# Channel sums of the RMS norms and of RWKV's bonus: data as weights against a matrix of ones as weights

## The chip, the cores and the metric

One NeuronCore of one Trainium2 chip runs the whole program. The metric is the device time of one execution in microseconds (us), as the median of several runs.

## The reference

The input x has 256 tokens of 1024 channels. Two layers follow one another. In each layer the input is RMS-normalised and modulated by a condition vector, and one combined projection feeds three branches whose gated outputs are merged, projected and added to x:

```
h = rms_norm(x, norm_pre) * (1 + scale) + shift
p = h @ w_in
o_mla  = attention on two RMS-normalised compressed projections (512 and 256 channels)
o_rwkv = RWKV-7: delta-rule state over heads of 64 channels, then
         y = group_norm(y) * ln_w + ln_b
         bonus = sum over a head's 64 channels of (r * k * r_k), times v
         y = y + bonus
o_gla  = gated linear attention, 4 heads of 256 value channels, each RMS-normalised
merged = sigmoid(gate_a)*o_mla + sigmoid(gate_b)*o_rwkv + sigmoid(gate_c)*o_gla
x = x + gate * rms_norm(merged @ w_out, norm_post)
```

## The kernel before

Activations stand channel-major: 128 channels in the partitions, the 256 tokens along a row. A weight matrix comes by DMA in tiles of 128x1024 float32 (`weights`, L333). ScalarE rounds each tile to a part `hi` that one TensorE pass carries exactly (L344), VectorE subtracts to get the rest `lo` (L345), and `dense` (L349) makes three products hi*hi, hi*lo, lo*hi for each 128x128 block (L358). `dense_pair` does this for 256 output columns. These products are most of TensorE's work.

The program is written layer by layer: RWKV's preparation `rw_prep` for half of the heads (L463), RWKV's chain over eight chunks of 32 tokens `rw_chain` (L562), GLA (`gla`, L821), `rw_prep` and `rw_chain` for the other half, MLA (`mla`, L910), and `finish` (L1069). The TileContext is opened with `schedule_with_timeline_sim=True`: when the program is built, a scheduler orders the instructions of each engine by a timing model of its own, and each engine then runs its list strictly in that order. So parts that stand far apart in the source run side by side (GLA beside the first chain, MLA beside the second), and an instruction that has to wait holds up all that stands behind it in its engine's list. PSUM has eight banks in three pools: `ps_d` (3, dense products), `ps_c` (2, RWKV's chain), `ps_m` (3, everything else).

At the head of a chain stands a triangular solve. `gram` products (L574) are masked into `Gm` (L581), go through DRAM (`bd`, `Bb`, L591 to L598), and GpSimd solves 31 columns, each by a product `tm` and a sum `Xb` (L607, L610). `Xb` goes through DRAM (`xd`, `Xs`, L612 to L618; ScalarE issues these DMAs) and the chain over the chunks can begin (`u`, L692).

Sums over channels, that is over partitions, are made by TensorE. Before, `sums` (L141) takes the data as the weights, 128 tokens at a time, and a column of ones (`one_b`), or two half columns (`halfsel`), as what moves: the result has tokens in the partitions and a column or two for each block of channels. The places:

- `start` (L268, once): 8 blocks of squares into `ss` (L281).
- `rw_prep` (L525 to L555, 4 times): 4 blocks into `bonp` (L535), copied to `bon` (L554). The sums of squares `ssk` (L517) are made in the same way.
- `gla` (L889, for each of 4 heads, in 2 layers): the head's squares `gsq`, whose two tiles GpSimd adds first (L888), into `gss`. After the last head come one square root, one reciprocal (L891, L892).
- `compress` in `mla` (L941): 2 blocks for the 512 channels (`cq`), 1 for the 256 (`ckv`), into `sscq` and `ssckv`; `rms_row` (L397) reduces them, takes the root and the reciprocal (L400 to L402).

To come back to channel-major, `to_rows` (L146) splits the result in two parts on VectorE (L149, L150), turns both on TensorE (L153, `ptr...`), copies the rows out on ScalarE (L157); and `spread` or `spread2` (L160, L164) multiplies a row by a column of ones so that it stands in all partitions (`ri`, `gbc`, `bc`; the PSUM results). `spread2` does so for the two heads of 64 channels in a tile. The consumers read that PSUM tile: `xn` (L285), `og` (L901), `cx` (L946), and at the end of a chain `bv` (L753), which GpSimd adds to `orw` (L755).

Of the kernel before, what the change touches and what calls it, by code (L numbers as in the profile page):

```python
# [20 lines left out]
P = 128  # L21
# [13 lines left out]
# Column slots of w_in, 256 columns each (see _w_in_columns).  # L35
# [7 lines left out]
# Columns of the packed per-channel parameters, one per 128 channels.  # L43
# [6 lines left out]
# Order of the column tiles of ada_w: shift and scale of the same channels side by side.  # L50
# [11 lines left out]
def _turn_pieces():  # L62
    """frac(2^k / 2 pi) for the steps of the pieces of an angle, each as a 12-bit part and the rest."""
    from fractions import Fraction

    pi = Fraction(314159265358979323846264338327950288419716939937510, 10 ** 50)
    out = []
    for k in (20, 9, -2):
        f = Fraction(2) ** k / (2 * pi)
        f -= round(f)  # L70
        hi = Fraction(round(f * 4096), 4096)
        out.append((k, float(hi), float(np.float32(float(f - hi)))))
    return out, float(np.float32(float(1 / (2 * pi))))
# [3 lines left out]
def trunk(  # L77
# [35 lines left out]
    pick = const.tile([16, 5], F32R, name="pick")  # L113
# [9 lines left out]
    # running sums start again at every 32nd or 64th token  # L123
# [12 lines left out]
    gneps = cut(1)  # L136
    A.copy(pick8, cut(8)[0:16].unsqueeze(2).broadcast_to([16, 8, 64]))
    A.copy(pick, cut(5)[0:16])
    pick4, pick1 = pick[0:8, 0:4], pick[0:2, 4:5]

    def sums(ps, src, sel):  # L141
        """ps [128, 2, n]: sums over channels of src [128, 256 tokens], tokens in the partitions."""
        for half in range(2):
            PE.matmul(ps[:, half], src[:, half * P:(half + 1) * P], sel, start=True, stop=True)

    def to_rows(pool, src, n, nm):  # L146
        """[2 n, 256]: src [128, 2, n], given for tokens, turned and in two parts that one pass carries."""
# [12 lines left out]
    def spread(ps, rows, j, sel):  # L160
        """ps [128 channels, 256] = row j, both parts."""
        PE.matmul(ps, sel[:, j:j + 1].broadcast_to([sel.shape[0], P]), rows, start=True, stop=True)

    def spread2(ps, rows, j):  # L164
        """Row j to the first 64 channels, the next to the others."""
# [81 lines left out]
    def interleave():  # L247
        """Part of the modulation that is wanted later, between two weight transfers."""
# [5 lines left out]
    def ada_part(L, l, slots, pool=None):  # L254
        """Two columns of the modulation for each slot, 128 channels each, before its bias."""
# [12 lines left out]
    def start(L, hl, firsts, order):  # L268
        """The first layer's input and its first products of it, 128 channels at a time as their
        modulation comes in."""  # L270
# [5 lines left out]
        ss = ps_m.tile([P, 2, KD], F32, tag="m", name="ss0")  # L276
        for s in range(4):
            sq = pp.tile([P, 2, T], F32, tag="sq", name="sq0", bufs=2)
            A.activation(sq, xn[:, 2 * s:2 * s + 2], AF.Square)
            for i in range(2):  # L280
                sums(ss[:, :, 2 * s + i:2 * s + i + 1], sq[:, i], one_b)  # L281
# [51 lines left out]
    def weights(src, name, n=2048, pool=None, sub=None):  # L333
        """Both parts of n columns of a slot, in tiles of CHUNK columns."""
# [14 lines left out]
    def dense(ps, w, kt, i, act):  # L349
        """ps [128 columns, 256 tokens] = W[:, column tile i].T @ activations; a tile's rows side by side."""  # L350
# [13 lines left out]
    def dense_tok(ps, w, kt, n, act, st):  # L364
        """ps [128 tokens, n columns] = activations.T @ W; a row's columns side by side."""
# [22 lines left out]
    def split(hi, lo, src, scale=None):  # L388
        """src (times scale) as the sum of two parts that one pass each carries exactly."""
# [7 lines left out]
    def rms_row(pool, ss, inv, nm):  # L397
        """[128, 256] 1 / rms of the tokens, in every partition; ss [128, 2, n] parts of the sums of squares."""
        r = pool.tile([P, 2, 1], F32, tag="rr", name=f"rr{nm}", bufs=2)
        V.tensor_reduce(r[:, :, 0], ss, AX.X, ALU.add)  # L400
        A.activation(r, r, AF.Sqrt, scale=inv, bias=eps6)
        V.reciprocal(r, r)  # L402
        rows = to_rows(pool, r, 1, nm)
        ps = ps_m.tile([P, T], F32, tag="m", name=f"ri{nm}")
        spread(ps, rows, 0, pick1)
        return ps

# [1 line left out]
    def norm_rows(pp, parts, nm):  # L409
        """1 / rms of the rows of a [128, 1024] given in parts."""  # L410
# [25 lines left out]
    def prenorm(L, hl, pp, xr, i):  # L436
        """128 rows of x, normalised and modulated, channel-major in two parts."""
# [4 lines left out]
        for half in range(2):  # L442
            ps = ps_c.tile([P, 4, P], F32, tag="c", name="ps_t")
            for k in range(4):
                # turned and normalised
# [17 lines left out]
    def rw_prep(L, l, qp, h, sh):  # L463
# [4 lines left out]
        R.GC = rw.tile([P, 4, 8], F32, tag="GC", name=f"GC{l}{qp}")  # L468
        n = f"{l}{qp}"
        with tc.tile_pool(name=f"rp{n}", bufs=1, side="right", reuse_waits="tile") as rp:  # L470
# [9 lines left out]
            for s in range(2):  # L480
# [5 lines left out]
                # two products at a time, in either half of the PE array's rows  # L486
# [38 lines left out]
            bonp = ps_m.tile([P, 2, 8], F32, tag="m", name="bonp")  # L525
            for s in range(2):
                g2 = slice(2 * s, 2 * s + 2)
                ps = dense_pair(win[l, S_RR[qp] + s], f"rr{n}{s}", h)
                br = rp.tile([P, 2, T], F32, tag="t2", name="br", bufs=3)
                for i in range(2):  # L530
# [4 lines left out]
                    sums(bonp[:, :, 2 * g:2 * g + 2], br[:, i], halfsel)  # L535
# [12 lines left out]
                # what the state loses comes first for the first pair of heads and last for the other  # L548
# [4 lines left out]
            bon = rp.tile([P, 2, 8], F32, name="bon")  # L553
            A.copy(bon, bonp)  # L554
            R.bon = to_rows(rw, bon, 8, f"bon{n}")  # L555
            for s in range(2):
                ps = dense_pair(win[l, S_RV[qp] + s], f"rv{n}{s}", h)
                for i in range(2):
                    shifted(L, R.vs[:, 2 * s + i], ps[:, i], "mu_v", qp * 4 + 2 * s + i)
        return R  # L560

    def rw_chain(L, l, qp, R, orw, rc):  # L562
        n = f"{l}{qp}"
        # A head is (gh, g2, qi).  Partitions of what is token-major: (g2, half, token of a chunk); the
        # removals of the pair of heads gh are in the half gh, its queries and values in the other.
        Gm = rc.tile([P, 8, 2, 2, 64], F32, name="Gm")
        for c4 in range(2):
            # heads in different rows of the PE array write different banks
# [16 lines left out]
        # The unit triangular systems of all chunks and heads of this half: one (row parity,  # L585
        # chunk, head) in each partition, solved column by column.
# [34 lines left out]
        # The states of two heads stand block-diagonally, as do the values.  # L621
# [12 lines left out]
        # four heads at a time, each in rows and columns of the PE array of its own  # L634
        pairs = [(g2, gh) for g2 in range(2) for gh in range(2)]

        def by_token(ch):
            """A chunk's decayed keys and its values, turned; the values into their blocks."""
# [23 lines left out]
        for ch in range(8):  # L662
# [4 lines left out]
            def of_state(ps, s):  # L667
                """What each pair's removals (s = 0) or queries read of the state."""
# [6 lines left out]
            def of_chunk(ps, s, r, g2, gh, qi):  # L675
                """... and of the chunk's tokens in the rows r."""
# [49 lines left out]
        # group norm over the 64 values of a head  # L726
# [21 lines left out]
        for s in range(2):  # L748
            bc = ps_c.tile([P, 2, T], F32, tag="c", name="bc2")
# [546 lines left out]
```

## Time and profile before

| | |
|---|---|
| three runs | 1183.28, 1189.07, 1191.8 us |
| median | 1189.07 us |
| span of the profiled execution, first to last instruction | 1181.3 us |
| TensorE matmul, weight load | 93%, 85% of the span |
| VectorE, ScalarE, GpSimd | 68%, 49%, 40% of the span |
| chain that ended last: TensorE, GpSimd, VectorE, DMA | 58%, 16%, 9%, 8% |

The profile names engines PE (TensorE matmuls), PEld (its weight loads, beside the matmuls), DVE (VectorE), ACT (ScalarE), POOL (GpSimd), SP (SyncE). A row of a group of instructions has line, engine, operation, out<-in, shapes, count, then busy us and mean ns of one, then the idle time before them. The profiled execution's own time is its span and what the launch puts around it; that is not listed apart, and the three runs lie 2.0 to 10.5 us above the span.

### The profile page before, as it was taken

What the parts mean: (1) busy time and instruction counts of PE and PEld (TensorE: products, weight loads), DVE (VectorE), ACT (ScalarE), POOL (GpSimd) and SP (SyncE); (2) the same over time, 40 slices, a digit from 0 to 9 for tenths busy, and PEclk for the clock granted to TensorE, in tenths of its full rate; (3) what the DMA queues carried; (4) which work ended last, traced back from release to release, by engine and by line L of the source; (5) the groups of instructions that cost most, each with busy time, mean ns of one, the idle gap of its engine ahead of it and who ended that gap; (6) DMA issues with size and microseconds to landing.
All of it is one profiled execution on the core that took longest, in us unless ns stands there. A gap on an engine that the chain in (4) does not pass through costs nothing.

```text
span 1181.3 us, 25207 instructions
## 1 busy us (share of the span) xinstructions
PE 1103.1 (93%) x10365; PEld 1001.9 (85%) x10365; DVE 799.6 (68%) x1220; ACT 578.8 (49%) x980; POOL 466.6 (40%) x609
## 2 busy tenths in 40 slices
PE   5799898999999599999989999899999969999997
PEld 3798887988999477999989889789899968799997
DVE  6978754766986667677665685367677665667774
ACT  4357233545547243554556834255384635446452
POOL 7955338324536643103100536523063753211210
PEclk7799998999999899999999989999999989999999
DMA  9665753465466443547654245334444542234761
GB/s 353 215 200 167 176 154 117 131 219 153 144 220 216 128 143 103 120 151 231 207 182 150 83 153 161 107 90 133 146 141 138 181 123 91 81 120 142 249 210 40
DMA packets 70066, 185.15 MB, mean 157 GB/s; under 512 B 24608, under 2 KB 25120, under 8 KB 69824
## 3 DMA queue, kind: packets, MB, share of 16 engines
q1 hardware_dynamic: 48304, 173.37, 46.3%
q10 hardware_dynamic: 21648, 10.18, 3.4%
q8 instruction: 81, 1.33, 0.5%
q14 instruction: 33, 0.27, 0.1%
HBM read 179.32 MB, written 4.20 MB: 155 GB/s over the span
## 4 chain that ended last, share of the span: by engine, by line
PE 58%; POOL 16%; DVE 9%; DMA 8%; issue 5%; ACT 4%; ACTq 1%; DVEq 0%; SPq 0%; POOLq 0%
PE ps_gt L358 10%; PE ps_wo L358 9%; POOL tm L607 5%; POOL Xb L610 5%; PE ps_rz L358 4%; PE y L371 3%; PE ps_gz L358 3%; PE ps_gq L358 2%; PE ps_mz L358 2%; PE ps_rk L358 2%; PE ps_rv L358 2%; DMA wr_wout<-in_wout_dram 2%; DMA Bb<-bd 1%; DMA adaw<-in_ada_dram 1%; PE sp L702 1%
## 5 line engine op out<-in xcount | busy, mean ns | idle before, releaser
L358 PE MATMUL ps_gt<-hhi,lo_gt 128*128 128x256 f32 x384 | 109.9, 286 | 0.1
L358 PE MATMUL ps_gt<-hhi,hi_gt 128*128 128x256 f32 x384 | 109.7, 286 | 0.0
L358 PE MATMUL ps_gt<-hlo,hi_gt 128*128 128x256 f32 x384 | 109.0, 284 | 0.0
L345 DVE TENSOR_TENSOR lo_gt<-wr_gt,hi_gt 128x1024 fp32r<-128x1024 f32 x48 | 63.4, 1322 | 40.1 <-ACT hi_gt L344 39.6
L345 DVE TENSOR_TENSOR lo_wo<-wr_wo,hi_wo 128x1024 fp32r<-128x1024 f32 x48 | 67.2, 1399 | 31.3 <-ACT hi_wo L344 31.1
L263 DVE SCALAR_TENSOR_TENSOR adaw<-adaw,cb 128x1024 f32<-128x1024 f32 x48 | 70.7, 1476 | 15.1 <-DMA adaw<-in_ada_dram 14.8
L344 ACT CAST hi_gt<-wr_gt 128x1024 fp32r<-128x1024 f32 x48 | 50.4, 1049 | 54.9 <-PE ps_gt L358 20.1
L344 ACT CAST hi_wo<-wr_wo 128x1024 fp32r<-128x1024 f32 x48 | 50.4, 1050 | 51.0 <-PE ps_gt L358 25.1
L358 PEld LDWEIGHTS ps_gt<-hhi,lo_gt 128*128 128x128 f32 x384 | 73.4, 191 | 1.5 <-DVE lo_gt L345 0.4
L358 PEld LDWEIGHTS ps_gt<-hhi,hi_gt 128*128 128x128 f32 x384 | 73.6, 192 | 1.0 <-issue 0.2
L712 POOL TENSOR_TENSOR gst<-ST,GC 64x256 f32<-64x256 f32 x48 | 39.0, 813 | 88.8 <-DVE ST L716 75.0
L358 PEld LDWEIGHTS ps_gt<-hlo,hi_gt 128*128 128x128 f32 x384 | 73.5, 191 | 0.6 <-issue 0.2
L607 POOL TENSOR_TENSOR tm<-Xb,Bb 128x126 f32<-128x126 f32 (+22 forms) x124 | 64.8, 523 | 22.9 <-DMA Bb<-bd 13.7
L785 POOL TENSOR_TENSOR merged<-merged,tg 128x512 f32<-128x512 f32 x14 | 24.6, 1758 | 122.6 <-DVE tg L784 108.9
L610 POOL TENSOR_TENSOR Xb<-Xb,tm 128x126 f32<-128x126 f32 (+22 forms) x124 | 61.0, 492 | 9.5
L643 POOL COPY bks<-vs 128x128 f32<-128x128 f32 x32 | 11.1, 346 | 131.4 <-PE ptok L650 125.4
L654 ACT COPY vals<-ptok 32x128 f32<-32x128 f32 x128 | 32.9, 257 | 46.7 <-PE ptok L650 34.2
L344 ACT CAST hi_gz<-wr_gz 128x1024 fp32r<-128x1024 f32 x16 | 16.8, 1048 | 50.6 <-PE ps_gz L358 18.8
L696 DVE COPY vals<-u 32x128 f32<-32x128 f32 x128 | 36.5, 286 | 7.0 <-PE u L692 5.1
L371 PE MATMUL ps_gv<-hi_gv,hhi 128*128 128x256 f32 x128 | 36.5, 289 | 3.4 <-ACT hi_gv L344 2.3
L358 PE MATMUL ps_gz<-hhi,hi_gz 128*128 128x256 f32 x128 | 39.6, 309 | 0.0
L358 PE MATMUL ps_gz<-hhi,lo_gz 128*128 128x256 f32 x128 | 39.3, 307 | 0.0
(492 smaller groups left out, 4358.9 us busy)
## 6 DMA issues: line engine op xcount, KB each, us to landing
adaw<-in_ada_dram SPq DMA_DIRECT2D x48, 512.0 KB, 3.8
wr_gt<-in_win_dram SPq DMA_DIRECT2D x48, 512.0 KB, 3.9
wr_wo<-in_wo_dram SPq DMA_DIRECT2D x48, 512.0 KB, 3.8
wr_rk<-in_win_dram SPq DMA_DIRECT2D x16, 512.0 KB, 5.1
wr_rr<-in_win_dram SPq DMA_DIRECT2D x16, 512.0 KB, 4.5
wr_rv<-in_win_dram SPq DMA_DIRECT2D x16, 512.0 KB, 4.2
wr_gv<-in_win_dram SPq DMA_DIRECT2D x16, 512.0 KB, 4.4
wr_gz<-in_win_dram SPq DMA_DIRECT2D x16, 512.0 KB, 4.2
```

What stands on the lines that cost most here:

```text
L263: V.scalar_tensor_tensor(w, w, 0.5, cb, ALU.mult, ALU.mult, accum_out=L.mod[:, ADA_ORDER[2 * s + i]:ADA_ORDER[2 * s + i] + 1],)
L344: A.copy(hi, wr)
L345: (sub or V).tensor_sub(lo, wr, hi.bitcast(F32))
L358: PE.matmul(ps if len(a.shape) == 2 else ps.rearrange("p (a b) -> p a b", a=2), wt[:, at + k * P:at + (k + 1) * P], a, start=i == 0, stop= ...
L371: PE.matmul(ps, a[:, st * P:(st + 1) * P] if len(a.shape) == 2 else a[:, st], wt[:, k * n % CHUNK:k * n % CHUNK + n], start=i == 0, stop=i ...
L607: G.tensor_mul(tv, Xb[:, 0:nr, m:m + 1].broadcast_to([P, nr, w]), Bb[:, m:m + 1, m + 1:32].broadcast_to([P, nr, w]))
L610: G.tensor_add(Xb[:, 0:nr, m + 1:32], Xb[:, 0:nr, m + 1:32], tv)
L654: A.copy(vals[ch % 2][rows(g2, 1 - gh), :, gh, g2], pt[32 * g:32 * g + 32, 2].rearrange("p (q v) -> p q v", q=2))
L696: V.tensor_copy(val[rows(g2, gh), :, gh, g2], u[rows(g2, gh)])
L702: PE.matmul(sp[chan(qi), 2 * gh:2 * gh + 2].rearrange("p g v -> p (g v)"), tk[:, gh, chan(qi)], val[:, qi, gh].rearrange("p g v -> p (g v) ...
L712: G.tensor_mul(gst[chan(qi)], ST[chan(qi), :, qi], R.GC[chan(qi), :, ch:ch + 1].broadcast_to([64, 4, 64]))
L785: (V if b == 2 and s == 3 else G).tensor_add(m, m, tg)
```

## The change

Two square matrices stand ready as weights: `ones`, all ones, and `twos`, block-diagonal ones in two blocks of 64. The new `all_sums` takes them as weights and the data, 256 tokens, as what moves. The result has the sum in every channel (or in the 64 channels of its head) at once, so that turning and spreading fall away. Per-row roots and reciprocals become 128x256 ones, and `rms_row` returns an SBUF tile instead of a PSUM one. In GLA each head has its own root and reciprocal, made inside the loop over heads. In `rw_prep` the bonus sums are copied to `R.bon`, 128x512 at a time, and GpSimd multiplies them by the values at the end of `rw_prep`; the end of the chain only adds them. The squares of the keys (`ssk`, `rn`) still go by `sums`, `to_rows` and `spread2`. Comments are dropped.

```diff
-    pick = const.tile([16, 5], F32R, name="pick")
+    ones = const.tile([P, P], F32, name="ones")
+    G.memset(ones, 1.0)
...
+    twos = const.tile([P, P], F32, name="twos")
+    A.copy(twos.rearrange("p (a b) -> p a b", a=2), halfsel.unsqueeze(2).broadcast_to([P, 2, 64]))
     A.copy(pick8, cut(8)[0:16].unsqueeze(2).broadcast_to([16, 8, 64]))
-    A.copy(pick, cut(5)[0:16])
-    pick4, pick1 = pick[0:8, 0:4], pick[0:2, 4:5]
...
+    def all_sums(ps, src, sel, first=True, last=True):
+        PE.matmul(ps, sel, src, start=first, stop=last)
...
-    def spread(ps, rows, j, sel):
-        PE.matmul(ps, sel[:, j:j + 1].broadcast_to([sel.shape[0], P]), rows, start=True, stop=True)
...
-        ss = ps_m.tile([P, 2, KD], F32, tag="m", name="ss0")
+        ss = ps_m.tile([P, T], F32, tag="m", name="ss0")
...
-                sums(ss[:, :, 2 * s + i:2 * s + i + 1], sq[:, i], one_b)
+                all_sums(ss, sq[:, i], ones, s + i == 0, s + i == 4)
...
-    def rms_row(pool, ss, inv, nm):
-        r = pool.tile([P, 2, 1], F32, tag="rr", name=f"rr{nm}", bufs=2)
-        V.tensor_reduce(r[:, :, 0], ss, AX.X, ALU.add)
-        A.activation(r, r, AF.Sqrt, scale=inv, bias=eps6)
+    def rms_row(pool, ss, inv, nm, bufs=2):
+        r = pool.tile([P, T], F32, tag="rr", name=f"rr{nm}", bufs=bufs)
+        A.activation(r, ss, AF.Sqrt, scale=inv, bias=eps6)
         V.reciprocal(r, r)
-        rows = to_rows(pool, r, 1, nm)
-        ps = ps_m.tile([P, T], F32, tag="m", name=f"ri{nm}")
-        spread(ps, rows, 0, pick1)
-        return ps
+        return r
...
+        R.bon = rw.tile([P, 4, T], F32, tag="bon", name=f"bon{l}{qp}")
...
-            bonp = ps_m.tile([P, 2, 8], F32, tag="m", name="bonp")
             for s in range(2):
...
+                bonp = ps_m.tile([P, 2, T], F32, tag="m", name="bonp")
                 for i in range(2):
...
-                    sums(bonp[:, :, 2 * g:2 * g + 2], br[:, i], halfsel)
+                    all_sums(bonp[:, i], br[:, i], twos)
+                A.copy(R.bon[:, g2], bonp)
...
-            bon = rp.tile([P, 2, 8], F32, name="bon")
-            A.copy(bon, bonp)
-            R.bon = to_rows(rw, bon, 8, f"bon{n}")
             for s in range(2):
                 ps = dense_pair(win[l, S_RV[qp] + s], f"rv{n}{s}", h)
                 for i in range(2):
                     shifted(L, R.vs[:, 2 * s + i], ps[:, i], "mu_v", qp * 4 + 2 * s + i)
+                g2 = slice(2 * s, 2 * s + 2)
+                G.tensor_mul(R.bon[:, g2], R.bon[:, g2], R.vs[:, g2])
...
         for s in range(2):
-            bc = ps_c.tile([P, 2, T], F32, tag="c", name="bc2")
-            for i in range(2):
-                spread2(bc[:, i], R.bon, 2 * (2 * s + i))
-            bv = rc.tile([P, 2, T], F32, tag="vb", name="bv", bufs=2)
-            V.tensor_mul(bv, R.vs[:, 2 * s:2 * s + 2], bc)
             o = orw[:, qp * 4 + 2 * s:qp * 4 + 2 * s + 2]
-            G.tensor_add(o, o, bv)
+            G.tensor_add(o, o, R.bon[:, 2 * s:2 * s + 2])
...
-        ss = ps_m.tile([P, 2, 4], F32, tag="m", name="gss")
+        rns = []
...
-            sums(ss[:, :, hd:hd + 1], sq[:, 0], one_b)
-        rn = gp.tile([P, 2, 4], F32, name="grn")
-        A.activation(rn, ss, AF.Sqrt, scale=1.0 / 256, bias=eps6)
-        V.reciprocal(rn, rn)
-        rn = to_rows(gp, rn, 4, f"g{l}")
+            ss = ps_m.tile([P, T], F32, tag="m", name="gss")
+            all_sums(ss, sq[:, 0], ones)
+            rns.append(rms_row(gp, ss, 1.0 / 256, f"g{l}{hd}", 4))
...
-            bc = ps_m.tile([P, T], F32, tag="m", name="gbc")
-            spread(bc, rn, hd, pick4)
             for dt in range(2):
-                V.scalar_tensor_tensor(o[:, dt], o[:, dt], L.p("gla_norm", dt), bc, ALU.mult, ALU.mult)
+                V.scalar_tensor_tensor(o[:, dt], o[:, dt], L.p("gla_norm", dt), rns[hd], ALU.mult, ALU.mult)
...
-                ss = ps_m.tile([P, 2, npair], F32, tag="m", name=f"ss{nm}")
+                ss = ps_m.tile([P, T], F32, tag="m", name=f"ss{nm}")
...
-                    sums(ss[:, :, s:s + 1], sq[:, 0], one_b)
+                    all_sums(ss, sq[:, 0], ones, s == 0, s == npair - 1)
```

## Rows read from the trace of the kernel before

**Rows 1.** The page: busy time of each engine; the chain by engine.
```profile
PE 1103.1 (93%) x10365; PEld 1001.9 (85%) x10365; DVE 799.6 (68%) x1220; ACT 578.8 (49%) x980; POOL 466.6 (40%) x609
...
PE 58%; POOL 16%; DVE 9%; DMA 8%; issue 5%; ACT 4%; ACTq 1%; DVEq 0%; SPq 0%; POOLq 0%
```
**Rows 2.** Stretches: length, busy of PE, PEld, DVE, ACT, POOL; granted clock; DMA.
```profile
20.00:30.00 10.00, 4.69 (x13) 2.76 (x13) 9.67 (x11) 3.09 (x4) 10.00 (x7) 0.50 0.99 372
...
200.00:210.00 10.00, 7.15 (x40) 6.95 (x39) 4.34 (x8) 7.26 (x9) 3.58 (x12) 0.68 0.49 146
...
400.00:410.00 10.00, 5.43 (x25) 4.86 (x26) 7.50 (x9) 2.61 (x4) 5.30 (x10) 0.58 0.23 71
...
960.00:970.00 10.00, 4.32 (x28) 3.57 (x29) 8.16 (x13) 4.60 (x10) 2.11 (x3) 0.57 0.52 132
```
**Rows 3.** The waits: total us, times, longest.
```profile
PE ps_uv L371 <- ACT kn L991: 11.5, 1, 11.5
...
ACT kn L991 <- POOL Xb L610: 11.7, 1, 11.7
...
PE gss L144 <- POOL gsq L888: 9.6, 3, 4.3
```
**Rows 4.** The chain in order of time, TensorE's small groups: start, us, what.
```profile
213.22 0.54 PE ptrg L153 x4
...
216.62 0.32 PE gbc L162
...
859.93 0.86 PE pw L489 x4
...
869.92 0.43 PE bc L166 x2
...
891.66 1.88 PE bonp L144 x16
...
897.12 0.54 PE ptrbon L153 x4
```
**Rows 5.** Groups of DVE by line and shape.
```profile
L901 DVE SCALAR_TENSOR_TENSOR og<-og,par,gbc 128x256 f32<-128x256 f32 x16 | 6.6, 474 | 1.6 <-PE gbc L162 1.6
...
L753 DVE TENSOR_TENSOR bv<-vs,bc 128x512 f32<-128x512 f32 x8 | 5.4, 680 | 0.0
...
L946 DVE SCALAR_TENSOR_TENSOR cx<-cx,par,ricq 128x256 f32<-128x256 f32 x8 | 3.3, 474 | 2.1 <-PE ricq L162 2.1
...
L523 DVE RECIPROCAL rn<-rn 128x16 f32<-128x16 f32 x4 | 1.0, 240 | 0.0
...
L892 DVE RECIPROCAL grn<-grn 128x8 f32<-128x8 f32 x2 | 0.4, 202 | 0.7 <-ACT grn L891 0.7
```
**Rows 6.** A group of ACT by line and shape.
```profile
L997 ACT COPY vm<-ps_uv 128x512 f32<-128x512 f32 x8 | 4.7, 587 | 2.0 <-PE ps_uv L371 2.0
```
**Rows 7.** A group of POOL by line and shape.
```profile
L755 POOL TENSOR_TENSOR orw<-orw,bv 128x512 f32<-128x512 f32 x8 | 14.1, 1773 | 45.8 <-DVE bv L753 45.7
```
**Rows 8.** The timeline of POOL, three instructions: start, us, what.
```profile
320.27 1.63 POOL L551 TENSOR_TENSOR BK<-av,E 128x512 f32<-128x512 f32 x1
...
366.79 1.39 POOL L610 TENSOR_TENSOR Xb<-Xb,tm 128x81 f32<-128x81 f32 x1
...
381.47 0.45 POOL L610 TENSOR_TENSOR Xb<-Xb,tm 128x133 f32<-128x133 f32 x1
```
**Rows 9.** The timeline of DVE at the same three moments.
```profile
320.67 1.20 DVE L735 TENSOR_REDUCE var<-ysq 128x16 f32<-128x1024 f32 x1
...
366.77 1.21 DVE L345 TENSOR_TENSOR lo_uq<-wr_uq,hi_uq 128x1024 fp32r<-128x1024 f32 x1
...
381.03 0.86 DVE L946 SCALAR_TENSOR_TENSOR cx<-cx,par,rickv 128x256 f32<-128x256 f32 x2
```
**Rows 10.** The timeline of ACT at the root of GLA's norm.
```profile
205.25 1.28 ACT L891 ACT_TABLE_LOAD   x1
```
**Rows 11.** The chain between layer 0's two RWKV chains.
```profile
340.93 1.28 DVE bv L753 x2
```

## The prediction

> **What bounds the kernel now.** I read the page's engine rows first. TensorE is busy for 1103.1 of the 1181.3 us, so it stands still for 78 us in all, and it holds 58% of the chain that ended last; GpSimd holds 16%, VectorE 9% [rows 1]. So most of the time a microsecond taken from TensorE's list is a microsecond gained, and the question is where it isn't. The view by stretches shows that: in 20 to 30 us GpSimd is busy for all ten microseconds and TensorE for 4.69; at 200 to 210, 400 to 410 and 960 to 970 TensorE is busy for 7.15, 5.43 and 4.32, and the granted clock is 0.68, 0.58 and 0.57 there, that is, partly at the lower of its two levels, 1.2 GHz, right after the standstill [rows 2]. The waits name the cause: `ps_uv` waits 11.5 us for ScalarE's copy `kn`, which stands for 11.7 us behind `Xb`, the solve on GpSimd (ScalarE's list has the solve's DMA issue ahead of the copy); and three times `gss` waits for GpSimd's sum `gsq`, 9.6 us in all, with the solve's steps ahead of it [rows 3]. So there are two regimes: TensorE-bound for most of the span, and bound by GpSimd at the start and towards the end of the solves.
>
> **The change part by part.** The sum is made against the span.
>
> *The sums themselves.* In float32 a call is two records: the eight calls of `bonp` are sixteen records, 1.88 us on the chain, 0.235 a call. A call with 256 moving columns is priced by `pw`: four records, so two calls, took 0.86 us, 0.43 a call [rows 4]. There are 76 calls of `sums` that go (start 16, bonus 32, GLA 16, MLA 12) and 38 of `all_sums`: 17.9 us against 16.3. The difference, 1.6 us, I leave at nothing, since `pw` uses half of the rows and a full weight matrix may cost a little more.
>
> *Turning and spreading.* These leave TensorE's list without a successor. Turns: `ptrbon` 0.54 and `ptrg` 0.54, four and two of them, 3.2 us. Spreads: `bc` of the bonus, eight pairs at 0.43, 3.4 us; `gbc`, eight at 0.32, 2.6 us [rows 4]. That is 9.2 us, all on the chain as TensorE time or beside it in TensorE-bound stretches. MLA's four turns (2.2) and four spreads (priced as `gbc`, 1.3) lie inside the solves' stretches, where TensorE waits afterwards anyhow; I count them at nothing, and 3.5 us if that is wrong. Those of `start` lie where GpSimd is the bound: nothing. So this part gives 9.2 us; its ends are 0 and 14.3.
>
> *VectorE.* It loses eight products `bv` of 0.68 each, 5.4 us [rows 5], and 22 tiny casts and subtractions. It gains 13 reciprocals of 128x256 (start 1, GLA 8, MLA 4), for which there is no row. 16 elements took 240 ns and 8 took 202 [rows 5]: 4.75 ns per further element, so 202 + 248 x 4.75 = 1.38 us, 18 us in all. Bounds: at the pace of the 256-element product `og`, 0.47 us; all of the 240 ns growing with the elements, 3.8 us. I take 1.4, the line through two rows of the same operation. VectorE is busy for 68%, and eleven of the thirteen fall to stretches in which TensorE has other work or waits for the solve; so on its own I count this at nothing, and at up to 18 us without that cover. One `bv` pair, 1.28 us at 340.93, is on the chain between layer 0's two RWKV chains [rows 11]: 1.3 us gained once. What is late next there is the subtraction for MLA's weights, behind it in the list. The product read the last of the two `ps_c` banks that the next chain's `gram` needs, so up to this much is gained in each of four places, 5.1 us, and nothing if another wait ends there; I take the one that the chain shows.
>
> *ScalarE.* Eight copies of `R.bon` from PSUM, at 0.587 each [rows 6], and roots of 256 instead of 1 to 8 elements, below that price; ScalarE is busy for 49%, and these wait for nothing that others wait for: nothing. Without the cover it is 8 x 0.59 + 13 x 0.59, some 12 us.
>
> *GpSimd.* Eight products `R.bon` x `vs` of 128x512, priced as the addition of that shape, 1.77 us [rows 7]: 14.2 us more. They stand at the end of `rw_prep`, ahead of the solve in GpSimd's list, and wait for the values. What is queued behind them is the solve's clearing and its first step, which wait for the DMA of `Bb` in any case; for the addition of the same shape GpSimd had 45.8 us of idle time [rows 7]. So nothing; with the values late it is 2 x 1.77 in front of each of four solves, 14 us.
>
> *The operand that moves from PSUM to SBUF.* This speaks against the change. A step of the solve took 1.39 us at 366.79 while VectorE's subtraction of two SBUF tiles (1.21 us) ran from 366.77; a larger step at 381.47 took 0.45 us while VectorE's `cx`, one of whose operands is in PSUM, ran from 381.03 to 381.89 [rows 8, 9]. So a VectorE instruction with both tiles in SBUF stops GpSimd, 0.94 us for 1.21, and one with a PSUM operand doesn't. The change turns the second sort into the first: `cx` (12 of 0.474 us, 5.7 us, all inside solves), `og` (16 of 0.474; I guess half of them inside solves, since a head's root is now ready before the last head's, 3.8 us) and `xn` (4 at the price of `bv`, 0.68, 2.7 us, beside the start's busy GpSimd) [rows 5]. Of `cx` all counts; of the others, 6.5 us, half, since the solves of the GLA stage end less sharply: 8.9 us of VectorE time, times 0.94/1.21, makes 6.9 us of longer solves. Ends: 0 and 9.5.
>
> The Trainium skill ("SBUF — State Buffer", section "SBUF: two separate sides") says that VectorE and GpSimd share one pair of ports as an exclusive lock, taken by a VectorE instruction with two SBUF inputs or in a two-port mode. The two moments above agree; by the page alone all 12.2 us would count.
>
> Sum: -9.2 - 1.3 + 6.9 = -3.6 us, a span of 1177.7. The median of the three runs, 1189.07, lies 7.8 above the profiled span; the same change on it gives **1185.5 us**, 0.3% faster. A measurement of this kernel tells about 1% from no change, 12 us here, so this is a forecast of no difference that shows.
>
> **The rivals.**
>
> *A, faster: TensorE's saving passes whole.* 14.3 us off TensorE, the solves starting 1.28 us sooner in four places (5.1), and the port free whenever it is wanted: -19, 1170 us. For it: 93% busy. Against: the stretches around 400 and 960, where a solve decides [rows 2].
>
> *B, slower: reciprocals stop the solve as well.* If a 128x256 reciprocal blocks GpSimd as the subtraction does, 13 of 1.38 us cost 17.9 x 0.94/1.21 = 13.9 us, and with all 12.2 us of the moved operands (9.5) against the gains of 10.5 it is +13: 1202 us. To be slower by 12 us it needs a stop of about 1.3 us for each reciprocal. Against it: at 320.67 a VectorE reduction of one SBUF tile kept its 1.20 us inside a GpSimd product that took 1.63 from 320.27, below the mean 1.77 of such shapes [rows 7 to 9]: one input didn't stop it.
>
> *C, no saving: ScalarE's tables.* Each root that follows a tanh needs a table load, 1.28 us at 205.25 [rows 10], and the tanh behind it another. GLA's one root per layer becomes four. With three more pairs in each of two layers it is 12 x 1.28 = 15.4 us of ScalarE, which holds up the casts of the weights; if half reaches TensorE, -3.6 + 7.7 = +4: 1193 us. Against it: the first three heads' roots stand before the first tanh, with squares and copies alone around them. The Trainium skill ("ScalarE: Activation LUTs", section "Table sets: the hidden batching unit") asks for exactly the batching that is given up here.
>
> The new order is a rival to every sum: the scheduler lays out each engine's list anew, by its own model, and a step that lands behind a solve's DMA issue waits some 11 us [rows 3]. It acts in both directions and widens the range.
>
> **How the numbers follow.** Forecast 0.50, A 0.26, B 0.15, C 0.09. Likeliest: 1185.5, by itself 1177 to 1194. Range: 1170 (A) to 1201 (just short of B), with one in ten left out on either side. Faster by over 1%: most of A, and a tenth of the forecast, 0.27. Slower by over 1%: most of B, some of C and of the forecast, 0.18. Within 1%: 0.55.
>
> **What would show it right or wrong.** Right: `ptrbon`, `ptrg`, `gbc` and the bonus's `bc` gone and TensorE's busy time some 10 us down; an isolated `all_sums` at 0.43 us a call; reciprocals at about 1.4 us; steps of the solve above 1 us beside `cx`; the solves' stretches as long or a few us longer. B would show as steps of the solve that last as long as a reciprocal; C as more than two or three additional table loads. The forecast is wrong if the standstills of TensorE change by more than 8 us either way, whatever its list saves.

## The result, and the profile after

The changed kernel takes 1204.04 us (median of four runs, 1203.35 to 1205.04) against 1188.46 us of the kernel before, run beside it: a ratio of 1.0126, 95% interval 1.0095 to 1.0157. It is slower by about 1.3%; the forecast was 1185.5 and the range ended at 1201.

The page of the changed kernel, its engine row and its chain by engine, against [rows 1]:

```profile
PE 1097.1 (91%) x10216; PEld 996.2 (83%) x10216; DVE 810.5 (67%) x1191; ACT 578.9 (48%) x977; POOL 474.0 (39%) x618
...
PE 58%; POOL 16%; DMA 9%; DVE 7%; issue 5%; ACT 4%; ACTq 1%; DVEq 0%; SPq 0%; POOLq 0%
```

TensorE is busy for 6.0 us less, but the span is 21.3 longer, so it stands still for 105.5 us instead of 78.2. The shares of the chain hardly change. Busy time hides one more thing, the clock. Span and mean granted clock of the kernel before:

```profile
core 0: 1181.3 us, clock 0.966
```

and of the changed kernel:

```profile
core 0: 1202.6 us, clock 0.951
```

The mean over the span also counts the clock during standstills, so it falls when standstill grows and can't be multiplied with the busy time. Instead, each stretch of busy time is weighted by the clock granted in that stretch; the sum estimates what the list would take at full speed: 1076.2 us before, 1061.0 after. So a span has three parts: work at full speed, time lost to the lower clock (busy less work), and standstill. Before: 1076.2 + 26.9 + 78.2. After: 1061.0 + 36.0 + 105.5. The change takes some 15 us of work off TensorE; standstill takes back 27 and the clock 9. (The execution of before that was profiled was the fastest of its runs, 1183.28, and that of after an average one, so 5.7 of these 21.3 us are no part of the difference of medians, 15.6.)

Where TensorE waited, from the waits of the changed kernel (total us, times, longest), against [rows 3]:

```profile
PE gss L150 <- POOL gsq L882: 12.8, 3, 7.5
PE ps_uk L360 <- DVE rotb L915: 11.1, 1, 11.1
PE ssckv L150 <- POOL csq L930: 9.3, 1, 9.3
PE ps_lora L295 <- ACT hhi L393: 8.6, 1, 8.6
PE ps_uv L373 <- ACT vm L987: 7.8, 1, 7.8
```

The wait of `ps_uv` for `kn` has shrunk, but `ps_uk`, `ssckv`, `ps_lora` and a longer `gss` have come. The same in stretches of the changed kernel (columns as in [rows 2]):

```profile
200.00:210.00 10.00, 4.18 (x13) 2.66 (x14) 1.77 (x2) 0.47 (x1) 7.92 (x24) 0.56 0.24 87
210.00:220.00 10.00, 7.97 (x45) 6.49 (x45) 4.25 (x9) 5.22 (x7) 2.64 (x3) 0.50 0.24 55
...
950.00:960.00 10.00, 4.13 (x21) 3.95 (x22) 2.54 (x3) 1.94 (x3) 8.30 (x24) 0.55 0.21 75
```

At 200 TensorE stands still, then it works at the lower level, 1.2 GHz (a granted clock of 0.50), through the ten microseconds that follow; at 950 the clock is partly at that level too. The timeline of TensorE has the instruction that waited at 198, with its idle time in brackets, and two pairs of bonus sums:

```profile
205.82 1.22 PE L150 MATMUL gss<-gsq,ones 128*128 128x256 f32 x2 [7.50 <-POOL gsq L882]
...
911.55 1.13 PE L150 MATMUL bonp<-br,twos 128*128 128x256 f32 x4
915.06 1.13 PE L150 MATMUL bonp<-br,twos 128*128 128x256 f32 x4
```

The groups of VectorE by line and shape, against [rows 5]; then one of ScalarE and one of GpSimd, against [rows 6, 7]:

```profile
L403 DVE RECIPROCAL rrg<-rrg 128x256 f32<-128x256 f32 x8 | 13.9, 1743 | 2.6 <-ACT rrg L402 2.6
...
L891 DVE SCALAR_TENSOR_TENSOR og<-og,par,rrg 128x256 f32<-128x256 f32 x16 | 10.2, 678 | 0.0
...
L936 DVE SCALAR_TENSOR_TENSOR cx<-cx,par,rrcq 128x256 f32<-128x256 f32 x8 | 3.3, 477 | 0.0
```

```profile
L535 ACT COPY bon<-bonp 128x512 f32<-128x512 f32 x8 | 4.7, 581 | 4.4 <-PE bonp L150 4.4
```

```profile
L558 POOL TENSOR_TENSOR bon<-bon,vs 128x512 f32<-128x512 f32 x8 | 13.1, 1640 | 41.7 <-DVE vs L459 23.9 <-ACT bon L535 17.9
```

### The profile page after: what moved, and what is told of

Read it like the earlier page. It is cut to its first block, busy times and chain, and to the rows that moved or that the text cites. A ratio compares the mean times of both kernels' runs of the same rounds, so it can differ in the third digit from the quotient of the medians.

```text
span 1202.6 us, 24898 instructions
## 1 busy us (share of the span) xinstructions
PE 1097.1 (91%) x10216; PEld 996.2 (83%) x10216; DVE 810.5 (67%) x1191; ACT 578.9 (48%) x977; POOL 474.0 (39%) x618
## 4 chain that ended last, share of the span: by engine, by line
PE 58%; POOL 16%; DMA 9%; DVE 7%; issue 5%; ACT 4%; ACTq 1%; DVEq 0%; SPq 0%; POOLq 0%
PE ps_gt L360 11%; PE ps_wo L360 10%; POOL Xb L609 5%; POOL tm L606 5%; PE ps_rz L360 4%; PE y L373 3%; PE ps_rv L360 2%; PE ps_rk L360 2%; PE ps_mz L360 2%; DMA Bb<-bd 2%; PE ps_gv L373 2%; DMA wr_wout<-in_wout_dram 2%; PE ps_rr L360 1%; PE ps_gz L360 1%; PE ps_gq L360 1%
## 5 line engine op out<-in xcount | busy, mean ns | idle before, releaser
L347 DVE TENSOR_TENSOR lo_gt<-wr_gt,hi_gt 128x1024 fp32r<-128x1024 f32 x48 | 63.0, 1314 | 34.2 <-ACT hi_gt L346 33.4
L606 POOL TENSOR_TENSOR tm<-Xb,Bb 128x126 f32<-128x126 f32 (+22 forms) x124 | 60.9, 491 | 33.2 <-DMA Bb<-bd 24.0
L609 POOL TENSOR_TENSOR Xb<-Xb,tm 128x126 f32<-128x126 f32 (+22 forms) x124 | 63.7, 514 | 9.6
L360 PE MATMUL ps_gz<-hlo,hi_gz 128*128 128x256 f32 x128 | 39.3, 307 | 0.0
```

Of the source, the lines that this page charges most:

```text
L347: (sub or V).tensor_sub(lo, wr, hi.bitcast(F32))
L360: PE.matmul(ps if len(a.shape) == 2 else ps.rearrange("p (a b) -> p a b", a=2), wt[:, at + k * P:at + (k + 1) * P], a, start=i == 0, stop= ...
L606: G.tensor_mul(tv, Xb[:, 0:nr, m:m + 1].broadcast_to([P, nr, w]), Bb[:, m:m + 1, m + 1:32].broadcast_to([P, nr, w]))
L609: G.tensor_add(Xb[:, 0:nr, m + 1:32], Xb[:, 0:nr, m + 1:32], tv)
```

## The experiments

Ratios are to the kernel before, run on the same chip beside them, with the 95% interval. Theories: **W**, TensorE waits for sums that stand on GpSimd behind the solve; **R**, the reciprocals cost what they take on VectorE; **G**, the bonus products hold up the solves; **O**, an edit makes the scheduler lay out the engines' lists anew, and the new order costs. **F** (the opposite of O): the work itself costs.

### The parts, one at a time

Each is the kernel before with one part of the change, in the form of the diff above.

> The kernel before with RWKV's bonus alone changed. W (norms' sums wait on GpSimd behind steps of the solve): the bonus is no part of the loss and saves its turns, spreads and bv, about 1178 us (-10). G (the products R.bon x vs and the copies hold up the solves' starts): 1195 to 1202. R (the reciprocals cost what they take on VectorE): no reciprocals here, so about 1180. O (any edit reorders the lists, and the time with them): anywhere from 1175 to 1204, with standstills at places that the edit doesn't touch.

> The kernel before with the norm of GLA's heads alone changed. W: TensorE waits for gsq behind the solve, as in the changed kernel (12.8 us against 9.6 before), and the clock falls after it; with ScalarE's and VectorE's lists held by the roots 1195 to 1205. R: 8 reciprocals of 1.74 are 13.9 us more on VectorE, 1195 to 1203, with VectorE as the releaser of TensorE's waits, not GpSimd. G: 1186, the saved turns and spreads. O: any time, standstills elsewhere too.

> The kernel before with the norms of MLA's compressed projections alone changed. W: ssckv waits for csq behind the solve's steps some 9 us in a layer, 1194 to 1200. R: 4 reciprocals are 7 us, 1190 to 1195. G: 1185 to 1188. O: any time.

> The kernel before with the start's norm alone changed; all lists behind it stay in the old order (four rows of TensorE's list differ). If the start is a loss of its own (root and reciprocal of 256 columns delay the first cast, the 6 us of standstill that the changed kernel has there): 1193 to 1197. If what it loses comes from lists that the whole change draws anew: 1188 to 1191, no difference.

Measured: `bonus_only` 1191.63 us, 1.0007 (0.998 to 1.0034); `gla_only` 1214.06, 1.0195 (1.0171 to 1.0219); `mla_only` 1182.25, 0.9921 (0.9892 to 0.9951); `start_only` 1191.98, 1.003 (0.9994 to 1.0066). G falls: the products cost nothing that shows. But the 10 us that W and R let the bonus save don't show either, though TensorE's list there has 7 us less work at full speed than before (1069.0 against 1076.2); and `mla_only` is faster than W, R and G each allowed. `start_only` does not decide between its two forecasts. A loss comes with GLA's part. W and R both forecast one there, but of at most 1205, half of what was measured; both were put to the test.

### Less on GpSimd, more on VectorE

The additions of the two halves of the squares leave GpSimd; TensorE accumulates both halves instead. `after_sum_pe` does so in the whole changed kernel, for MLA's squares too; `gla_sum_pe` has GLA's part alone. The edit in GLA:

```diff
-            G.tensor_add(sq[:, 0], sq[:, 0], sq[:, 1])
             ss = ps_m.tile([P, T], F32, tag="m", name="gss")
-            all_sums(ss, sq[:, 0], ones)
+            for half in range(2):
+                all_sums(ss, sq[:, half], ones, half == 0, half == 1)
```

> The changed kernel with both halves of the squares summed on TensorE (two accumulating products in place of GpSimd's addition and one product). W: the waits of gss and ssckv for GpSimd go (22 us with half of what follows them given back at other ends), 14 products of 0.43 come in, so 1180 to 1192. R: the reciprocals stay, so 1204 plus up to 6 = 1204 to 1210. G: as R. O: any time, but the waits for gsq and csq are gone all the same.

> GLA's norm alone changed (which took +1.95%), with both halves of the squares summed on TensorE, so that nothing of the sums stands on GpSimd behind the solve. W (the wait of gss for gsq, and the half clock after it, is the loss): most of the 23 us go, 1188 to 1198; what is left is the solve's own end. R (the reciprocals, 8 of 1.74 us on VectorE): they stay, 1210 to 1217. O (the order by chance): any time between 1185 and 1215, though the waits for gsq are gone.

Measured: `after_sum_pe` 1192.96 us, 1.0025 (1.0003 to 1.0048), a microsecond above W's 1180 to 1192; `gla_sum_pe` 1209.26, 1.0155 (1.0106 to 1.0205), well above W's 1198 and just below R's 1210. The profile of `gla_sum_pe` shows why W fails there. TensorE's timeline, and ScalarE's:

```profile
214.79 1.65 PE L149 MATMUL gss<-gsq,ones 128*128 128x256 f32 x3 [10.35 <-ACT gsq L897]
```

```profile
210.68 0.33 ACTq L623 DMA_DIRECT2D xd<-Xb  x1
211.13 1.04 ACT L349 CAST hi_gt<-wr_gt 128x1024 fp32r<-128x1024 f32 x1 [13.70 <-POOL Xb L621]
212.71 1.39 ACTq L627 DMA_DIRECT2D Xs<-xd  x2
214.15 0.60 ACT L897 ACTIVATE gsq<-po 128x512 f32<-128x512 f32 x1 [1.97 <-issue]
```

The square `gsq` now stands on ScalarE behind the DMA issue that waits for the solve, and TensorE waits longer than before, 10.35 us. One wait went and another list made a new one. In `after_sum_pe` no wait of `gss` or `ssckv` is left, but TensorE waits longer for the solve's result, against 2.5 us in the changed kernel:

```profile
PE u L691 <- DMA Xs<-xd: 26.0, 4, 10.8
```

For R each of GLA's reciprocals was done three times (the value is the same; `rms_all` is the name that `rms_row` of the change has in kernels with a part of it):

```diff
             rns.append(rms_all(gp, ss, 1.0 / 256, f"g{l}{hd}", 4))
+            for _ in range(2):
+                V.reciprocal(rns[-1], rns[-1])
```

> GLA's norm alone changed, each reciprocal done three times over (the value stays the same): 16 more of 1.74 us, 27.8 us more on VectorE. R: each costs what it takes or a good part of it, 1225 to 1242. W: VectorE has room for them, 1212 to 1220. O: anywhere, also faster than 1214.

Measured: `gla_recip3` 1210.0 us, 1.0159 (1.0129 to 1.0189). The added group on VectorE:

```profile
L904 DVE RECIPROCAL rrg<-rrg 128x256 f32<-128x256 f32 x16 | 27.9, 1744 | 0.0
```

27.9 us more on VectorE, and the time is not longer than that of `gla_only`; no wait of TensorE in this trace ends at a reciprocal. R falls.

The additions were also taken off GpSimd in the kernel before (the two halves accumulated by the old one-column products), and in GLA alone together with MLA's new norms:

> The kernel before, nothing of the change, with GpSimd's additions gsq and csq taken out and both halves summed on TensorE by the old products of one column. W: the waits for gsq (9.6 us) and the half clock behind them go, in part given back at the solve's end: 1176 to 1186. R: no reciprocals are touched, 1189 to 1190 as before. O: any time.

> MLA's norms as changed (which alone took -0.8%), GLA's and the bonus as before, and GLA's two halves summed on TensorE. If the parts add up and W holds, 1182 less what before_sum_pe gains in GLA: 1170 to 1180. R: 1182, as MLA alone. O: any time.

Measured: `before_sum_pe` 1204.56 us, 1.0103 (1.0063 to 1.0142), and `mla_new_gla_old_pe` 1197.15, 1.004 (1.0013 to 1.0066). W falls as the cause: the old kernel without those waits is slower by 1%, with nothing of the change in it. In the first the waits for `gsq` are gone, and a longer one has come behind them, for the root of GLA's norm, which ScalarE's list now has behind the solve's DMA issues:

```profile
PE ptrg L153 <- DVE hlg L150: 7.8, 1, 7.8
```

### Controls: the same work in another order

In the first, two lines of GLA change places:

```diff
-            A.activation(sq, po, AF.Square)
             V.tensor_copy(og[hd // 2][:, 2 * (hd % 2):2 * (hd % 2) + 2], po)
+            A.activation(sq, po, AF.Square)
```

> A control: the kernel before with two program lines of GLA swapped (VectorE's copy of a head's output ahead of ScalarE's square of it), no work added, removed or resized; the scheduler lays out about a third of TensorE's list and a fifth of ScalarE's and VectorE's otherwise. O (the lists' order, which any edit of GLA draws anew, moves the time, by standstills and by the half clock behind them): more than 0.5% from the kernel before, most likely slower, 1195 to 1212, with the sum of standstill and half clock 8 to 25 us higher. F (GLA's norm costs time by what it is): within 0.4% of before, 1186 to 1194.

> A second control: the kernel before with one buffer instead of two for the bonus's product bv; the same instructions in another order (a tenth of TensorE's list). O: 0.3 to 1.5% from before, either way, 1180 to 1207. F: within 0.4%, at most 1.3 us a chain more by the one buffer.

> A third control: the kernel before with two groups of lines of MLA's rotated key swapped, no work changed; some 6% of TensorE's list in another order, all in MLA. O: 0.2 to 1% either way, 1180 to 1200, from the MLA stages alone. F: within 0.3%.

Measured: `before_og_first`, GLA's lines, 1206.52 us, **1.0155** (1.0118 to 1.0191); `before_vb1`, the buffer, 1188.11, 0.9986 (0.9965 to 1.0007); `before_krb_first`, the rotated key, 1192.65, 1.0022 (1.0001 to 1.0042). Span and clock, and the engine row, of the first:

```profile
core 0: 1203.6 us, clock 0.953
```

```profile
PE 1117.7 (93%) x10365; PEld 1016.0 (84%) x10365; DVE 802.7 (67%) x1220; ACT 580.0 (48%) x980; POOL 467.4 (39%) x609
```

As many instructions as before, to the last one on TensorE, and the same work (1073.9 us, against 1076.2 before; five kernels with these same instructions on TensorE give 1072.9 to 1076.2 in this estimate). The 16 us are order alone: lost clock 43.8 instead of 26.9, standstill 85.9 instead of 78.2. A wait for the solve's result in the kernel before; then two of TensorE's waits in this control:

```profile
PE u L692 <- DMA Xs<-xd: 10.5, 2, 9.0
```

```profile
PE u L692 <- DMA Xs<-xd: 16.4, 2, 11.2
PE gss L144 <- POOL gsq L888: 13.7, 5, 6.3
```

The wait of `gss` was 9.6 us before, and the wait of 11.5 us for `kn` [rows 3] is gone: the waits behind the solve have changed places. This settles that order alone can make a loss of the size of the whole change's. The two edits away from GLA's loop, which reorder less of the lists, move little: for the buffer O had forecast at least 0.3%, and F was right; for the rotated key both allowed what came. So it is not any edit that costs.

GLA's stretch in layer 1, from its last `ps_gk` to the first `ps_gt`, in the kernel before, in this control, and in the changed kernel (columns as in [rows 2]):

```profile
720.86:791.33 70.47, 66.14 (x631) 58.05 (x629) 33.83 (x58) 27.89 (x46) 35.50 (x69) 0.98 0.33 100
```

```profile
737.03:815.70 78.67, 68.61 (x677) 59.90 (x675) 37.27 (x66) 29.08 (x51) 38.48 (x76) 0.96 0.31 95
```

```profile
732.29:812.98 80.69, 71.94 (x642) 61.95 (x640) 47.05 (x71) 30.40 (x51) 41.22 (x81) 0.87 0.31 92
```

70.5 us has become 78.7 by the swap and 80.7 by the change; standstill (length less PE busy) has gone from 4.3 to 10.1 and 8.8, and in the changed kernel the clock from 0.98 to 0.87. Over all kernels run, the two GLA stretches together take 162.7 to 169.2 us in the nine that leave GLA's head loop alone, the kernel before among them, and 174.6 to 189.9 us in the eleven that edit it in any way, all eleven of them slower than before (1.0025 to 1.0195). The shortest of the eleven, 174.6, is the control; whether the changed work adds to what its order costs there is not shown.

### Pairs: the change under the same edit

Does the change gain or lose once both kernels are drawn anew? Three more edits were made to the changed kernel and one more to the kernel before: the same two lines swapped, the lines of the rotated key swapped, and the DMAs `xd` and `Xs` issued by SyncE instead of ScalarE.

> The changed kernel with the same two lines of GLA swapped as in the first control. O: its time moves by 0.3 to 1.5% from the changed kernel's 1204, so 1186 to 1215; a time at or below 1190 would mean that the loss of 1.3% belongs to that one order and not to the change. F: 1200 to 1208.

> The changed kernel with the solve's result issued by SyncE instead of ScalarE. If ScalarE's list is the carrier: the waits for vm, kn and (in part) rotb go, about 20 us in all, of which half shows, 1190 to 1198. If SyncE's list is held instead: 1205 to 1230, with waits for weights. O: any time.

> The kernel before with the solve's result issued by SyncE instead of ScalarE; its partner with the change is after_sp, 1.0103. If the change itself gains some 0.7% once both are drawn anew: 1.012 to 1.022, 1204 to 1216. If it loses by what it is: 0.995 to 1.003, 1184 to 1194. O says only that it differs from before by more than 0.3%.

> The changed kernel with the two groups of lines of MLA's rotated key swapped; its partner without the change is before_krb_first, 1.0022. If the change itself gains some 0.7%: 0.99 to 1.0, 1178 to 1190. If it loses by what it is: 1.010 to 1.018, 1202 to 1212. O: 0.99 to 1.02, and different from the changed kernel's 1.0126 by more than 0.3%.

| edit to both | old: ratio; work, clock, standstill | changed: ratio; work, clock, standstill | difference |
|---|---|---|---|
| none | 1; 1076.2, 26.9, 78.2 | 1.0126; 1061.0, 36.0, 105.5 | +1.26% |
| GLA's lines | 1.0155; 1073.9, 43.8, 85.9 | 1.0085 (1.0055 to 1.0115); 1060.6, 29.8, 105.7 | -0.70% |
| halves on TensorE | 1.0103; 1080.8, 40.1, 81.3 | 1.0025; 1066.8, 28.2, 96.1 | -0.78% |
| SyncE issues | 1.0041 (1.0012 to 1.007); 1074.6, 43.7, 75.7 | 1.0103 (1.0046 to 1.0159); 1055.5, 45.3, 95.2 | +0.62% |
| rotated key | 1.0022; 1075.4, 33.4, 80.4 | 1.0092 (1.006 to 1.0123); 1057.6, 40.8, 98.8 | +0.70% |

Two things are the same in all five pairs: TensorE's work falls by 13 to 19 us (mean 15.9), and its standstill grows by 15 to 27 (mean 20.0). The clock's part goes either way, from -14 to +9 us, and decides the sign in these traces. It is read from one execution of each kernel, and the kernel before alone ran with a mean clock of 0.950 to 0.966, in 1179 to 1199 us. The +0.62% of the third edit is within the noise of its two ratios; the other four differences are not. The forecasts of the last three runs are not met as a set: `after_sp`, 1198.48, lies just past the slow end of what ScalarE's list would give; `before_sp`, 1193.97, fits "loses by what it is" in microseconds and lies just above it as a ratio; `after_krb_first`, 1200.87, lies between "gains" and "loses". The mean of the five differences is +0.2%; these five spread over two per cent, so whether the change as such gains or loses up to a per cent stays open.

### Two combinations

> MLA's norms and the bonus changed, GLA's and the start's norms as before. If the parts add up: 1.0007 x 0.9921 = 0.993, 1180 to 1184. If the order rules: lists drawn anew in GLA's stretch as well, anywhere from 1178 to 1205, without a relation to the two parts alone.

> MLA's norms changed (0.992 alone), and the two transfers of the solve's result (xd, Xs) issued by SyncE instead of ScalarE. If ScalarE's list, held by the solve, makes the waits of ps_uk and ps_uv for vm and kn (11 us): they go, 1168 to 1180. If SyncE's list, now held by the solve, keeps weights waiting: TensorE waits for DMA of weights instead, 1185 to 1215. O: the order anew, any time.

Measured: `mla_bonus_both` 1187.67 us, 0.9996 (0.9969 to 1.0023), where addition gave 0.993; and `mla_sp` 1186.97, 0.9999 (0.9967 to 1.0031). The parts don't add up, though bonus, GLA and MLA (+0.07, +1.95, -0.79; with the start's +0.30 it is 1.53) add to nearly the whole's 1.26: that sum looks like luck. And ScalarE's list is not the one carrier: freed of the solve's issues, neither MLA's part nor the changed kernel (`after_sp`) gains clearly. `mla_only`, 0.8% faster than before, is the best kernel measured, but its gain did not survive either companion, so whether it comes from its order or from its work is not shown.

## Why the prediction was wrong

**The step that failed is the last sentence of the rivals**, that the new order "acts in both directions and widens the range". One wrong place was priced, some 11 us, but the new order got no term in the sum, no chance and no direction. Its size is now measured: with no work changed, -0.1% to +1.55%, and for edits of GLA's loop, of which the change is one, up in every case. The row to learn from stood in the prediction itself: a wait of 11.5 us [rows 3] is what one wrong place in a list costs, and the clock that falls behind a standstill adds to it (26.9 us of lost clock beside 78.2 of standstill before, 43.8 beside 85.9 in the control). The prediction's own sign of being wrong came: the standstills changed by 27.3 us, where 8 was the bound. A forecast should have asked what the present order is worth, since it cannot be kept.

**"Most of the time a microsecond taken from TensorE's list is a microsecond gained"** is wrong here. The list lost some 16 us in the mean of the five pairs, more than the 9.2 counted and about the 14.3 of rival A, and 20 us of standstill came in its place. What the change itself touches was counted well: weighted in the same way, its turns and spreads fell by 11.6 us from one trace to the other, and the sums grew by 2.5; the rest of the fall is in products that were not touched. 93% busy is an average; GLA, MLA and the preparations run beside a solve and a chain that TensorE has to wait for, and there its other work fills waiting time. That this is how the saving went is argued from the stretches; that it went is shown by the five pairs.

**The sums:** a call of `all_sums` took 0.56 us (1.13 for two), not 0.43: 38 of them make 21 us where the old 76 calls were counted at 17.9. A small loss instead of the small gain; right to count at nothing.

**The reciprocals:** 1.74 us, not 1.38. The line through two short ones was too flat: (1743 - 202) / 248 is 6.2 ns per further element instead of 4.75. The estimate's use, that VectorE hides them, held: 27.9 us more of them cost nothing that shows.

**The moved operand:** mis-sized, 6.9 us where next to nothing came. The four solves, first `tm` to last `Xb` in the timelines, took 148.2 us before and 147.1 after. Two things were wrong. First, the overlap: before, all twelve `cx` ran beside steps of a solve, and the prediction kept them there; in the changed kernel three of twelve did, and five of the sixteen `og`. VectorE's timeline has four `cx` that end as the solve's first step starts, at 946.49:

```profile
944.96 1.66 DVE L936 SCALAR_TENSOR_TENSOR cx<-cx,par,rrcq 128x256 f32<-128x256 f32 x4
```

Second, the price. The timelines of GpSimd and VectorE in the changed kernel, at a short two-operand instruction:

```profile
963.42 0.50 POOL L606 TENSOR_TENSOR tm<-Xb,Bb 128x136 f32<-128x136 f32 x1
```

```profile
962.98 1.23 DVE L936 SCALAR_TENSOR_TENSOR cx<-cx,par,rrckv 128x256 f32<-128x256 f32 x2
```

The two `cx`, 0.6 us each, had both inputs in SBUF now, and the step beside them took 0.50 us; with no such instruction beside it, it takes 0.44 (the next fence). All the solve's steps that ran beside an `og` or a `cx`, and beside no subtraction, add up to some 0.6 us above the shortest step of their shape. The stop had been scaled by length, 0.94 us for 1.21; a step pays only for what is left of the VectorE instruction when it starts (the last section). Part of the cost fell on the other side: `og` went from 474 ns [rows 5] to 678.

**Rival B** falls too: beside a reciprocal the solve's steps keep their pace, 0.44 and 0.46 us in GpSimd's timeline while the reciprocal ran from 190.10:

```profile
190.21 0.44 POOL L606 TENSOR_TENSOR tm<-Xb,Bb 128x136 f32<-128x136 f32 x1
190.73 0.46 POOL L609 TENSOR_TENSOR Xb<-Xb,tm 128x136 f32<-128x136 f32 x1
```

```profile
190.10 1.73 DVE L403 RECIPROCAL rrg<-rrg 128x256 f32<-128x256 f32 x1
```

B's number, 1202, came near the result by luck: the mechanism does not show in the trace. **Rival C** falls: 31 table loads after, 33 before. **Bonus:** hidden, as counted; its copy took 0.58 us and its product 1.64, beside 0.587 and 1.77.

## What to carry to other kernels

Where a scheduler lays out the lists, a tuned kernel's order is part of its speed, and an edit of a loop that runs beside the bottleneck can throw it away, as eleven of eleven did here: make a control that changes the order and no work before you credit or blame the work. Split the span into work at full speed, lower clock and standstill, with the clock taken where the engine is busy; if work falls and standstill rises by as much, the list that was shortened was not what set the time. An edit that saves one or two per cent of an engine's work can't be judged from one order.

## What the runs showed of the hardware

The stop that a VectorE instruction with two SBUF inputs puts on GpSimd is not proportional to its length, as the prediction had it. It lasts to that instruction's end. In the changed kernel 25 steps of a solve ran beside just one of the subtractions, `cx` or `og` that had begun before them and had over 0.16 us left; each was longer than the shortest step of its shape by what was left, less 0.13 to 0.14 us. That makes 0.86 to 1.07 us beside the weights' subtractions, which lasted 1.2 to 1.5 us, 0.33 beside one of 128x512, and 0.06 to 0.08 beside `cx` and `og`. A step that was itself running when a subtraction began, and that no earlier one held, lasted at most 0.02 us longer than the shortest. And several in a row don't let GpSimd in between. The timeline of GpSimd in the changed kernel, first a step of 31 elements as it usually is, then one at the start of layer 1's second solve:

```profile
173.79 0.24 POOL L606 TENSOR_TENSOR tm<-Xb,Bb 128x31 f32<-128x31 f32 x1 [3.25 <-DMA Bb<-bd]
...
946.49 3.70 POOL L606 TENSOR_TENSOR tm<-Xb,Bb 128x31 f32<-128x31 f32 x1 [7.85 <-DMA Bb<-bd]
```

and VectorE's at that moment:

```profile
946.54 1.22 DVE L347 TENSOR_TENSOR lo_uq<-wr_uq,hi_uq 128x1024 fp32r<-128x1024 f32 x1
947.68 1.28 DVE L394 TENSOR_TENSOR cqlo<-cx,cqhi 128x512 fp32r<-128x512 f32 x2
948.88 1.22 DVE L347 TENSOR_TENSOR lo_uq<-wr_uq,hi_uq 128x1024 fp32r<-128x1024 f32 x1
```

Four VectorE instructions with two SBUF inputs follow one another to 950.1, and the step of 0.24 us ends at 950.2. The Trainium skill ("SBUF — State Buffer", section "SBUF: two separate sides") calls the shared ports a lock that whoever starts first holds for a whole instruction; the 25 steps above agree, and so do the one-input reciprocals, which stay out of it. The trace adds one case in which VectorE kept it over four instructions while GpSimd waited.
